# Hybrid layer in fp32: a chunk ahead in the feed-forward part, the first norm's residual on TensorE, w_out's last chunk by token halves

## The chip, the cores and the metric

The kernel runs on one core of a Trainium2 chip. The metric is the device time of one execution in microseconds (us). The engines are TensorE (PE; its weight loads PEld), VectorE (DVE), ScalarE (ACT), GpSimd (POOL) and SyncE (SP). DMAs are asked for on the queues of SP, ACT and POOL.

## The reference

One token batch of 256 tokens, model width 2048, feed-forward width 5632, all in fp32. Cut to what matters:

```python
def _mixer(x, w_in, ...):
    parts = jnp.split(x @ w_in, cuts, axis=-1)
    ...    # dilated attention -> ya; gated linear attention -> o
    ya = ya.reshape(b, s, A_WIDTH) @ w_proj_a
    o = o * lax.rsqrt(jnp.mean(o * o, axis=-1, keepdims=True) + LN_EPS) * gla_norm_g
    yb = (o.reshape(b, s, G_DV) * jax.nn.silu(gr)) @ w_proj_b
    y = jax.nn.sigmoid(m_a) * ya + jax.nn.sigmoid(m_b) * yb
    return y @ w_out

def _conv_ffn(x, w_gate, w_up, conv_w, conv_b, w_down):
    ...    # gc: 3-tap convolution of g = x @ w_gate over the tokens
    return (jax.nn.silu(gc) * (x @ w_up)) @ w_down

x = _layernorm(ALPHA * x + mix, ln1_g, ln1_b)
x = _layernorm(ALPHA * x + ffn, ln2_g, ln2_b)
```

## The kernel before

**Weights.** All weights come in pieces of 1 MB (128x2048, fp32), loaded by SP into `raw` (2 buffers) or `quarter` (6 buffers). `two_parts` splits a piece into two fp32r numbers: ScalarE writes the high one (`whi`, L136, 3 buffers) and VectorE the low one (`wlo`, L137, 2 buffers). TensorE then makes three products for each block of the operand: high by high, low by high and high by low (L228, L230 and L244, L247 for tiles; L260 to L262 for chunks). Every engine takes its instructions in order, so a split that stands behind something that waits is late, and TensorE with it.

**Units.** `seven` (L315) makes a block product with seven products instead of eight. It needs sums of weight pieces, made by accumulating DMAs on POOL's queue (`add_by_dma`, L345), or for the first v unit on VectorE (`add`, L342), and sums of operand quarters (`combine`, L292, instructions L301 to L304 on VectorE and their splits).

**Order.** The code is written as one list of work in which side work (attention, gates, sums) is dealt out by `pump` between weight pieces. A scheduler then fixes each engine's order before the run, from dependences and buffers; blocks of 128x512 come from one pool tag `blk`, with 14, 17 and 8 buffers in the pools early, late and last.

**The stages that the change touches.** (1) The v units run early. (2) In the late pool, `gated_out` (L830 to L840) makes sigmoid(gr) * gr * o for each head and both token halves and transposes the result for w_proj_b (L807), beside the product `yp` by w_proj_a. (3) `wo` is the product by w_out in four chunks of 512 columns, 16 operand blocks each, for both token halves; each chunk is followed by the residual (L902) and statistics (L903). (4) The first norm: mean and scale (L887 to L892), four products `keep` (L907), normalise (L915), 32 transposes (L923), gain and offset (L926), the operand split (L928, L931). The normalised `r` and the finished transposed `x1f` are spilled to DRAM. (5) The feed-forward part has six parts of 8, 8, 8, 8, 8 and 4 tiles of 128 columns. Part 0 runs as two groups of tiles (`fg`, `fu`, convolution L948 to L962), the next as one unit (`fgu`, four tiles) and one group. The unit of part p+1 is interleaved with the eight `step`s of the down-projection of part p: four chunks n of 512 columns with two weight pieces each, into the banks `wd_t` of both halves. A chunk's running sum `af` is fetched from DRAM at its first step (ACT's queue), added by `more` (L1029) and spilled (POOL's queue). In part 0, what is fetched is the normalised `r`, and `more` first applies the norm's gain and offset by two broadcast rows for each n (`row`, POOL's queue, and L1028 on VectorE).

## Time and profile before

| | |
|---|---|
| timed runs, median (lowest to highest) | 1941.08 us (1939.01 to 1942.84), 3 runs |
| the profiled execution's own time | 1931.08 us |
| its span | 1929.3 us |
| granted TensorE clock over the span | 0.981 |
| DMA moved | 480.45 MB, mean 249 GB/s |
| normalise, L915 on ScalarE | 8 of 0.80 us |
| weight splits on VectorE, L137 from quarter | 250 of 2.287 us |

How to read the rows that follow: a timeline row holds the start in us, the length in us, engine, line, operation, what is written <- what is read, shape, how many instructions of the kind follow each other, and in brackets how long the engine was idle before it and what ended that. A row of a group holds the count, then the busy time in us, the mean of one in ns, and the idle time before them by what ended it. A row of a DMA group holds the queue that issued it, the count, the size and the median time from issue to landing. Times count from the start of the span.

### The profile page before, as it was taken

The page shows a single profiled execution, that of the slowest core. Times are in us where ns is not written, and L with a number is a line of the kernel's source. Part 1 is how long each engine was busy: PE and PEld are TensorE (multiplying, and loading weights), DVE is VectorE, ACT ScalarE, POOL GpSimd, SP SyncE. Part 2 cuts the span into 40 slices and gives each one's busy share as a digit, 9 for nine tenths or more (in the row PEclk, how much of TensorE's full clock was granted, in tenths as well). Part 3 has the DMA queues.
Part 4 walks back from the last instruction along what each step waited for, and adds up shares of the span by engine and source line. Part 5 has one row for each costly group of instructions (what it writes and reads, how often), then busy time and mean ns, then how long its engine had stood idle before and what let it go on. Part 6 is the DMA issues. An engine that isn't in the chain of part 4 may idle for free.

```text
span 1929.3 us, 22786 instructions
## 1 busy us (share of the span) xinstructions
PE 1829.9 (95%) x8910; PEld 1523.0 (79%) x8910; DVE 1433.8 (74%) x1269; ACT 1020.0 (53%) x979; POOL 166.1 (9%) x270
## 2 busy tenths in 40 slices
PE   8989999999999999999999989887999999998996
PEld 6778887888888888887888868765887887887875
DVE  6979878878878797855755566675785786776877
ACT  6556555556665666545633345543554554554552
POOL 0001000001100111003100010010010000000101
PEclk9999999999999999999999989988999999999998
DMA  8469997987978879777765276668579587686783
GB/s 315 166 266 264 304 331 196 307 294 219 341 231 283 314 221 334 228 294 267 276 215 195 88 284 219 179 201 284 186 225 337 170 251 303 195 287 260 218 272 142
DMA packets 94920, 480.45 MB, mean 249 GB/s; under 512 B 11841, under 2 KB 22108, under 8 KB 46300
## 3 DMA queue, kind: packets, MB, share of 16 engines
q1 hardware_dynamic: 50252, 345.06, 47.6%
q0 software_dynamic: 22960, 107.08, 22.1%
q10 hardware_dynamic: 21600, 26.85, 4.3%
q8 instruction: 70, 1.15, 0.2%
q14 instruction: 38, 0.31, 0.0%
HBM read 385.55 MB, written 35.82 MB: 218 GB/s over the span
## 4 chain that ended last, share of the span: by engine, by line
PE 75%; DMA 10%; DVE 6%; issue 6%; ACT 2%; POOL 0%; SPq 0%; ACTq 0%; DVEq 0%; POOLq 0%
PE qk L228 8%; DMA raw<-in_wp 5%; PE fu L228 4%; PE qk L230 4%; DVE wlo L137 3%; PE fg L228 3%; PE wd_t L261 3%; PE wd_t L260 3%; PE wd_t L262 3%; PE fguD L329 2%; PE fu L230 2%; PE gqk L228 2%; PE fguA L329 2%; PE fg L230 2%; PE mD L329 2%
## 5 line engine op out<-in xcount | busy, mean ns | idle before, releaser
L137 DVE TENSOR_TENSOR wlo<-quarter,whi 128x2048 fp32r<-128x2048 f32 x250 | 571.0, 2287 | 182.3 <-ACT whi L136 73.1
L136 ACT ACTIVATE whi<-quarter 128x2048 fp32r<-128x2048 f32 x250 | 478.5, 1917 | 383.6 <-DVE quarter L342 89.5
L136 ACT ACTIVATE whi<-raw 128x2048 fp32r<-128x2048 f32 (+1 forms) x167 | 314.5, 1885 | 323.8 <-DMA raw<-in_wp 135.8
L137 DVE TENSOR_TENSOR wlo<-raw,whi 128x2048 fp32r<-128x2048 f32 (+1 forms) x167 | 375.8, 2250 | 123.5 <-ACT whi L136 52.8
L228 PE MATMUL qk<-x,whi 128*128 128x512 f32 x768 | 193.0, 399 | 1.5 <-ACT whi L136 1.5
L228 PEld LDWEIGHTS qk<-x,whi 128*128 128x128 f32 x768 | 142.0, 188 | 32.5 <-ACT whi L136 2.2
L342 DVE TENSOR_TENSOR quarter<-quarter,quarter 128x2048 f32<-128x2048 f32 x64 | 146.0, 2284 | 0.5
L261 PE MATMUL wd_t<-wlo,h 128*128 128x512 f32 x352 | 139.4, 396 | 5.6 <-DVE wlo L137 5.6
L260 PE MATMUL wd_t<-whi,h 128*128 128x512 f32 x352 | 138.2, 396 | 1.7 <-DVE af L1029 1.5
L262 PE MATMUL wd_t<-whi,h 128*128 128x512 f32 x352 | 138.3, 393 | 0.0
L345 POOL DMA_DIRECT2D quarter<-quarter x56 | 49.3, 880 | 665.5 <-DMA quarter<-in_wp 185.9
L230 PEld LDWEIGHTS qk<-x,wlo 128*128 128x128 f32 x768 | 98.4, 191 | 4.0 <-DVE wlo L137 0.3
L230 PE MATMUL qk<-x,wlo 128*128 128x256 f32 x768 | 99.7, 283 | 0.0
L228 PE MATMUL fu<-x,whi 128*128 128x512 f32 x368 | 89.7, 397 | 8.4 <-DVE pa L948 8.4
L228 PE MATMUL fg<-x,whi 128*128 128x512 f32 x352 | 88.0, 404 | 8.8 <-DVE af L1029 8.7
L228 PEld LDWEIGHTS fu<-x,whi 128*128 128x128 f32 x368 | 68.9, 192 | 22.3 <-issue 7.2
L228 PEld LDWEIGHTS fg<-x,whi 128*128 128x128 f32 x352 | 67.3, 196 | 23.4 <-issue 5.2
L261 PEld LDWEIGHTS wd_t<-wlo,h 128*128 128x128 f32 x352 | 67.1, 191 | 23.3 <-DVE wlo L137 9.4
L260 PEld LDWEIGHTS wd_t<-whi,h 128*128 128x128 f32 x352 | 67.0, 190 | 16.8 <-ACT h L136 1.7
L262 PEld LDWEIGHTS wd_t<-whi,h 128*128 128x128 f32 x352 | 67.0, 190 | 13.8
L228 PE MATMUL gqk<-x,whi 128*128 128x512 f32 x256 | 65.9, 407 | 4.4 <-ACT whi L136 4.1
L228 PEld LDWEIGHTS gqk<-x,whi 128*128 128x128 f32 x256 | 49.3, 196 | 17.7 <-ACT whi L136 7.7
(359 smaller groups left out, 3103.8 us busy)
## 6 DMA issues: line engine op xcount, KB each, us to landing
raw<-in_wp SPq DMA_DIRECT2D x163, 1024.0 KB, 5.1
quarter<-in_wp SPq DMA_DIRECT2D x160, 1024.0 KB, 11.1
quarter<-quarter POOLq DMA_DIRECT2D x56, 1024.0 KB, 12.2
af<-acc ACTq DMA_DIRECT2D x40, 256.0 KB, 13.0
acc<-af POOLq DMA_DIRECT2D x40, 256.0 KB, 5.2
sp<-c POOLq DMA_DIRECT2D x14, 256.0 KB, 10.6
bias<-bvd ACTq DMA_DIRECT2D x32, 96.0 KB, 4.8
v<-vs ACTq DMA_DIRECT2D x24, 128.0 KB, 2.9
```

The source lines that it names most:

```text
L136: nc.scalar.activation(hi, src, AF.Copy)
L137: nc.vector.tensor_tensor(lo, src, hi.bitcast(F32), op=ALU.subtract)
L228: nc.tensor.matmul(ps, parts(kc)[0], opnd(kc), start=(kc == 0), stop=False)
L230: nc.tensor.matmul(ps[:, S:], parts(kc)[1], opnd(kc)[:, :S], start=False, stop=(kc == nk - 1))
L260: nc.tensor.matmul(ps, xh, hi, start=first, stop=False)
L261: nc.tensor.matmul(ps, xh, lo, start=False, stop=False)
L262: nc.tensor.matmul(ps, xl, hi, start=False, stop=last)
L329: nc.tensor.matmul(ps, a(kc)[which], w[:, k * 512 : (k + 1) * 512], start=(first and w is hi and which == 0 and kc == 0), stop=(w is lo an ...
L342: tt(a, a, b, op=ALU.add)
L345: nc.gpsimd.dma_start(a, b, accum_op=ALU.add)
```

## The change

- **Sums.** In `combine` the operand quarters are got by a function; in the feed-forward part the getting of the blocks (`x1p`, four DMAs of 128x256 for each j) and the sums are two turns of the side work, and the turns are dealt out from the fourth tile of the first group on, not the eighth.
- **v.** The sums of weight pieces of the first v unit are accumulating DMAs too.
- **gated_out** is cut in three turns: fetch of head i, products of head i-1, transposes of head i-2.
- **w_out.** The last chunk runs by token halves: all four pieces are split first, then 48 matmuls for t=0 and 48 for t=1, each half followed by its norm (`normalised`). `keep` stands ahead of the second half's transposes. A spilled `x1f` is now 128x4x128 of one half; `r` is not spilled.
- **Residual.** In part 0 of the down-projection, TensorE adds the residual to `wd_t`: 8 fp32 matmuls for each n, x1f by `weighted`, which is ALPHA times the identity. `more` there is a copy of the bank on ScalarE and a spill. Rows and gain and offset on VectorE go.
- **Ahead.** `ahead(n + 1)` fetches a chunk's blocks at the first step of the chunk before.

```diff
@@ -296,7 +296,7 @@
...
             f = [tmp("comb").rearrange("p (k t) -> p k t", k=2) for _ in range(4)]
-            (a11, a21), (a12, a22) = ([raw[h][:, :, t * P : (t + 1) * P] for t in range(2)] for h in (j, j + 4))
+            (a11, a21), (a12, a22) = ([raw(h, t) for t in range(2)] for h in (j, j + 4))
             tt = nc.vector.tensor_tensor
@@ -405,11 +405,11 @@
...
     make_identity(nc, ident)
+    weighted = cpool.tile([P, P], F32, name="weighted")
+    nc.vector.tensor_scalar(weighted, ident, ALPHA, None, op0=ALU.mult)
     prm = cpool.tile([P, NPAR], F32, name="prm")
...
     pc = lambda c: prm[:, c : c + 1]
-    ones = cpool.tile([P, P], F32, name="ones")
-    nc.gpsimd.memset(ones, 1.0)
@@ -742,14 +742,14 @@
...
         for u in range(n):
-            yield from seven(name, X, comb, AT[name, u], sink(u), by_dma=(name, u) != ("v", 0))
+            yield from seven(name, X, comb, AT[name, u], sink(u), by_dma=True)
         yield lambda: passed.add(mark)
...
     next(tiles)()
-    comb, part = combine(X, XR)
+    comb, part = combine(X, lambda h, t: XR[h][:, :, t * P : (t + 1) * P])
     for j in range(4):
@@ -827,20 +827,31 @@
...
-    def gated_out(h):
+    got = {}
+    def gated_get(h):
+        got[h] = [(fetch("gr", GR[h][t]), fetch("o", O[h][t])) for t in range(2)]
+    def gated_mul(h):
+        for t, (x, o) in enumerate(got[h]):
+            sg = blk("sg")
+            nc.scalar.activation(sg, x, AF.Sigmoid)
+            nc.vector.tensor_tensor(x, x, o, op=ALU.mult)
+            nc.vector.tensor_tensor(sg, sg, x, op=ALU.mult)
+            got[h][t] = sg
+    def gated_stage(i):
         def f():
-            g = []
-            for t in range(2):
-                x, o = fetch("gr", GR[h][t]), fetch("o", O[h][t])
-                sg = blk("sg")
-                nc.scalar.activation(sg, x, AF.Sigmoid)
-                nc.vector.tensor_tensor(sg, sg, x, op=ALU.mult)
-                nc.vector.tensor_tensor(sg, sg, o, op=ALU.mult)
-                g.append(sg)
-            OB.extend(transposed("ob", h, g, P_NG))
+            if i < GH:
+                gated_get(i)
+            if 0 <= i - 1 < GH:
+                gated_mul(i - 1)
+            if 0 <= i - 2 < GH:
+                OB.extend(transposed("ob", i - 2, got[i - 2], P_NG))
         return f
-    side.extend(gated_out(h) for h in range(GH))
+    side.extend(gated_stage(i) for i in range(GH + 2))
     last_gate = []
@@ -892,44 +903,59 @@
...
+    def residual(n, t, ps):
+        r = R[t][n]
+        nc.vector.scalar_tensor_tensor(r, r, ALPHA, ps, op0=ALU.mult, op1=ALU.add)
+        nc.vector.bn_stats(stats[t][:, n, :], r)
+    X1 = [res("x1") for _ in range(4)]
+    X1F = [[None] * 4 for _ in range(2)]
+    def normalised(t):
+        _, rs, ms = mean_and_scale(t)
+        for n in range(4):
+            r = R[t][n]
+            nc.scalar.activation(r, r, AF.Identity, scale=rs, bias=ms)
+            pt = bank("pt")
+            x1 = blk("x1f").rearrange("p (k t) -> p k t", k=4)
+            for k in range(4):
+                nc.tensor.transpose(pt[:, k * P : (k + 1) * P], r[:, k * P : (k + 1) * P], ident)
+            for k in range(4):
+                d = 4 * n + k
+                nc.vector.tensor_scalar(x1[:, k], pt[:, k * P : (k + 1) * P], pc(P_L1G + d), pc(P_L1B + d), op0=ALU.mult, op1=ALU.add)
+            hi, lo = X1[n][:, :, t * P : (t + 1) * P], X1[n][:, :, S + t * P : S + (t + 1) * P]
+            main = nc.scalar.activation(hi, x1, AF.Copy)
+            nc.vector.tensor_tensor(lo, x1, hi.bitcast(F32), op=ALU.subtract)
+            X1F[t][n] = spill("x1s", x1)
+            if n == 2:
+                held = main
+        return held
+    yt = by_pairs(YT)
     for n in range(4):
...
             nc.gpsimd.dma_start(R[t][n], xk[t * P : (t + 1) * P, n * 512 : (n + 1) * 512])
-        pss = a_chunk("wo", by_pairs(YT), 16, AT["wo"] + 4 * n)
-        for t in range(2):
-            r = R[t][n]
-            nc.vector.scalar_tensor_tensor(r, r, ALPHA, pss[t], op0=ALU.mult, op1=ALU.add)
-            summed = nc.vector.bn_stats(stats[t][:, n, :], r)
-    norm = [mean_and_scale(t) for t in range(2)]
-    keep = bank("keep")
-    for _ in range(4):
-        nc.tensor.matmul(keep, ones, R[1][2], start=True, stop=True)
-    X1 = [res("x1") for _ in range(4)]
-    X1F = []
-    ACC = [[None] * 4 for _ in range(2)]
-    for n in range(4):
-        for t in range(2):
-            _, rs, ms = norm[t]
-            r = R[t][n]
-            nc.scalar.activation(r, r, AF.Identity, scale=rs, bias=ms)
-            ACC[t][n] = spill("acc", r)
-        for k in range(0, 4, 2):
-            pt = bank("pt")
-            x1 = blk("x1f")
-            for i in range(2):
-                for t in range(2):
-                    c = i * S + t * P
-                    nc.tensor.transpose(pt[:, c : c + P], R[t][n][:, (k + i) * P : (k + i + 1) * P], ident)
-                d = 4 * n + k + i
-                c = slice(i * S, (i + 1) * S)
-                nc.vector.tensor_scalar(x1[:, c], pt[:, c], pc(P_L1G + d), pc(P_L1B + d), op0=ALU.mult, op1=ALU.add)
-            hi, lo = X1[n][:, k : k + 2, :S], X1[n][:, k : k + 2, S:]
-            main = nc.scalar.activation(hi, x1.rearrange("p (k t) -> p k t", k=2), AF.Copy)
-            if n == 2:
-                held = main
-            nc.vector.tensor_tensor(lo, x1.rearrange("p (k t) -> p k t", k=2), hi.bitcast(F32), op=ALU.subtract)
-            X1F.append(spill("x1s", x1))
+        if n < 3:
+            pss = a_chunk("wo", yt, 16, AT["wo"] + 4 * n)
+            for t in range(2):
+                residual(n, t, pss[t])
+    pcs = [two_parts(load(AT["wo"] + 12 + k), spare=(k > 1)) for k in range(4)]
+    for t in range(2):
+        ps = cbank(f"wo_t{t}")
+        for k0 in range(4):
+            hi, lo = pcs[k0]
+            for k in range(4):
+                w = slice(k * 512, (k + 1) * 512)
+                kc = 4 * k0 + k
+                a_part(ps, yt(kc), hi[:, w], lo[:, w], t, kc == 0, kc == 15)
+        residual(3, t, ps)
+        if t:
+            keep = bank("keep")
+            for _ in range(4):
+                nc.tensor.matmul(keep, ident, R[0][2], start=True, stop=True)
+        held = normalised(t)
@@ -1017,16 +1044,21 @@
...
+        def ahead(n):
+            for t in range(2):
+                if part:
+                    st[n, t] = fetch("af", ACC[t][n], by=nc.scalar)
+                else:
+                    st[n, t] = fetch("x1f", X1F[t][n], lambda name: blk(name).rearrange("p (k t) -> p k t", k=4), by=nc.scalar)
         def more(n, pss):
             for t in range(2):
-                if last:
-                    a = F[t][:, n]
+                a = F[t][:, n] if last else st[n, t] if part else blk("wd0")
+                if part:
+                    nc.vector.tensor_tensor(a, a, pss[t], op=ALU.add)
                 else:
-                    a = st[n, t]
-                if not part:
-                    for i, op in ((2, ALU.mult), (3, ALU.add)):
-                        nc.vector.tensor_tensor(a, a, st["row", i], op=op)
-                nc.vector.scalar_tensor_tensor(a, a, 1.0 if part else ALPHA, pss[t], op0=ALU.mult, op1=ALU.add)
+                    nc.scalar.activation(a, pss[t], AF.Copy)
                 if last:
@@ -1037,17 +1069,21 @@
...
                     st["ps"] = [mbank(f"wd_t{t}") for t in range(2)]
+                    if n < 3:
+                        ahead(n + 1)
+                chunk_step(st["ps"], hk, nf, at, k0)
+                if not k0 and not part:
                     for t in range(2):
-                        st[n, t] = fetch("af", ACC[t][n], by=nc.scalar)
-                    if not part:
-                        for i in (2, 3):
-                            st["row", i] = row(i, n)
-                chunk_step(st["ps"], hk, nf, at, k0)
+                        for k in range(4):
+                            nc.tensor.matmul(
+                                st["ps"][t][:, k * P : (k + 1) * P], st[n, t][:, k], weighted, start=False, stop=False
+                            )
                 if k0 + 4 == nf:
...
         if not last:
+            ahead(0)
             return [step(n, k0) for n in range(4) for k0 in range(0, nf, 4)]
@@ -1067,14 +1103,18 @@
...
-    comb1, part1 = combine(X1, XF := {})
+    XF = {}
+    comb1, part1 = combine(X1, lambda h, t: XF[h, t])
     def sums(j):
-        def f():
+        def get():
             for h in (j, j + 4):
-                XF[h] = fetch("x1f", X1F[h], by=nc.scalar).rearrange("p (k t) -> p k t", k=2)
-            part1(j)
-        return f
+                pair = blk("x1p")
+                for t in range(2):
+                    b = pair[:, t * S : (t + 1) * S].rearrange("p (k t) -> p k t", k=2)
+                    nc.scalar.dma_start(b, X1F[t][h // 2][:, 2 * (h % 2) : 2 * (h % 2) + 2])
+                    XF[h, t] = b
+        return [get, lambda: part1(j)]
@@ -1084,11 +1124,11 @@
...
                     step()
+                    if not k and n == 3:
+                        side.extend(f for j in range(4) for f in sums(j))
                     if k or n > 3:
...
                             pump()
-                    if n == 7 and not k:
-                        side.extend(sums(j) for j in range(4))
         else:
```

In the unit of part 1, VectorE had the following before: the first chunk's residual instructions L1028 (on `af` and `row`) between the weight splits, and L1029 behind them.

```order
L137 TENSOR_TENSOR wlo_9507<-quarter_9420,whi_9506 128x2048
L1028 TENSOR_TENSOR af_9461<-af_9461,row_9465 128x512
L1028 TENSOR_TENSOR af_9463<-af_9463,row_9465 128x512
L137 TENSOR_TENSOR wlo_9523<-quarter_9422,whi_9522 128x2048
L1028 TENSOR_TENSOR af_9461<-af_9461,row_9467 128x512
L137 TENSOR_TENSOR wlo_9541<-raw_9538,whi_9540 128x2048
L1028 TENSOR_TENSOR af_9463<-af_9463,row_9467 128x512
L342 TENSOR_TENSOR quarter_9420<-quarter_9420,quarter_9578 128x2048
L342 TENSOR_TENSOR quarter_9422<-quarter_9422,quarter_9580 128x2048
L1029 SCALAR_TENSOR_TENSOR af_9461<-af_9461,wd_t_1128_9459 128x512
L1029 SCALAR_TENSOR_TENSOR af_9463<-af_9463,wd_t_1129_9460 128x512
```

Now, at the same place, the splits and the sums of weight pieces (L342) follow each other:

```order
L137 TENSOR_TENSOR wlo_9523<-quarter_9432,whi_9522 128x2048
L342 TENSOR_TENSOR quarter_9432<-quarter_9432,quarter_9592 128x2048
L137 TENSOR_TENSOR wlo_9539<-quarter_9434,whi_9538 128x2048
L342 TENSOR_TENSOR quarter_9434<-quarter_9434,quarter_9594 128x2048
L137 TENSOR_TENSOR wlo_9557<-raw_9554,whi_9556 128x2048
L137 TENSOR_TENSOR wlo_9602<-quarter_9432,whi_9601 128x2048
L137 TENSOR_TENSOR wlo_9618<-quarter_9434,whi_9617 128x2048
L137 TENSOR_TENSOR wlo_9643<-raw_9640,whi_9642 128x2048
```

The four L1028 and two L1029 rows are gone. On TensorE the residual stands behind the chunk's first weight piece, as products of `weighted` and the fetched blocks (two rows, one for each token half), ahead of the unit's next product `fguD`:

```order
L261 MATMUL wd_t_1123_9472<-wlo_9480,h_8727 128x512
L262 MATMUL wd_t_1123_9472<-whi_9479,h_8727 128x512
L1078 MATMUL wd_t_1122_9471<-weighted,x1f_9428 128x128 x4
L1078 MATMUL wd_t_1123_9472<-weighted,x1f_9430 128x128 x4
L329 MATMUL fguD_9521<-whi_9522,comb_1026_8598 128x512 x8
L329 MATMUL fguD_9521<-wlo_9523,comb_1026_8598 128x512 x4
```

On ScalarE the end of the second chunk of this down-projection is a copy of the two banks (L1061). The fetches of the blocks of the last chunk (L114) stand behind it, and weight splits (L136) before, between and behind:

```order
L136 ACTIVATE whi_9717<-raw_9715 128x2048
L136 ACTIVATE whi_9753<-quarter_9592 128x2048
L136 ACTIVATE whi_9769<-quarter_9594 128x2048
L1061 ACTIVATE wd_1149_9745<-wd_t_1138_9634 128x512
L1061 ACTIVATE wd_1151_9749<-wd_t_1139_9635 128x512
L114 DMA x1f_9788<-x1s_8469 128x512
L136 ACTIVATE whi_9794<-raw_9792 128x2048
L114 DMA x1f_9790<-x1s_8592 128x512
```

The copies were on VectorE as L1029; they now stand in the queue of the high splits. At the end of w_out TensorE had, before, the last matmuls of both halves, then keep and all transposes:

```order
L261 MATMUL wo_t_986_8326<-wlo_8420,yt_7913 128x512
L262 MATMUL wo_t_986_8326<-whi_8419,yt_7913 128x512
L907 MATMUL keep_8465<-r_8193,ones 128x512 x4
L923 MATMUL pt_8480<-ident,r_7931 128x128
L923 MATMUL pt_8492<-ident,r_7931 128x128
L923 MATMUL pt_8480<-ident,r_7933 128x128
```

Now a transpose group of the first half (four instructions, L923) stands between the matmuls of the second half (`wo_t_1009`):

```order
L261 MATMUL wo_t_1009_8471<-wlo_8338,yt_7657 128x512
L262 MATMUL wo_t_1009_8471<-whi_8337,yt_7657 128x512
L923 MATMUL pt_8412<-ident,r_7935 128x128 x4
L260 MATMUL wo_t_1009_8471<-whi_8337,yt_7657 128x512
L923 MATMUL pt_8427<-ident,r_8065 128x128 x4
L261 MATMUL wo_t_1009_8471<-wlo_8338,yt_7657 128x512
```

and behind the second half come keep, its transposes and the first feed-forward tiles:

```order
L260 MATMUL wo_t_1009_8471<-whi_8349,yt_7913 128x512
L261 MATMUL wo_t_1009_8471<-wlo_8350,yt_7913 128x512
L262 MATMUL wo_t_1009_8471<-whi_8349,yt_7913 128x512
L957 MATMUL keep_8522<-r_8195,ident 128x512 x4
L923 MATMUL pt_8535<-ident,r_7937 128x128 x4
L923 MATMUL pt_8550<-ident,r_8067 128x128 x4
L923 MATMUL pt_8565<-ident,r_8197 128x128 x4
L244 MATMUL fg_8620<-x_959_7931,whi_8604 128x512
L244 MATMUL fu_8621<-x_959_7931,whi_8610 128x512
```

So half of the transposes moved ahead of the last matmuls, and the first tiles `fg` and `fu` stand ahead of the last transpose group.

More of the change, by code (lines that the diff above doesn't have):

```diff
@@ L1012, in hybrid_layer @@
     F = []
+    ACC = [[None] * 4 for _ in range(2)]
     def down_group(part, nf, hs):
@@ L1115, in hybrid_layer @@
         older = down_group(part, nf, [h() for h in hs])
-    ACC = [[F[t][:, n] for n in range(4)] for t in range(2)]
     act_set(ACT_LN_EXP, held_by[0])
@@ L1121, in hybrid_layer @@
         for n in range(4):
-            a = ACC[t][n]
+            a = F[t][:, n]
             o = out[t * P : (t + 1) * P, n * 512 : (n + 1) * 512]
```

## The prediction

> **What bounds the kernel now.** I read the page first: span, busy shares, chain of work that ended last.
>
> ```profile
> span 1929.3 us, 22786 instructions
> PE 1829.9 (95%) x8910; PEld 1523.0 (79%) x8910; DVE 1433.8 (74%) x1269; ACT 1020.0 (53%) x979; POOL 166.1 (9%) x270
> PE 75%; DMA 10%; DVE 6%; issue 6%; ACT 2%; POOL 0%; SPq 0%; ACTq 0%; DVEq 0%; POOLq 0%
> ```
>
> TensorE is busy 1829.9 of 1929.3 us, so a change that removes no matmul can win at most the 99.4 us in which it idles, and the slow clock that follows an idle stretch. Next I read TensorE's timeline for rows with an idle time in brackets, around the lines that the diff touches.
>
> ```profile
> 906.20 0.66 PE L807 MATMUL pt<-ident,sg 128*128 128x128 f32 x2 [4.20 <-issue]
> 1118.71 0.39 PE L262 MATMUL wo_t<-whi,yt 128*128 128x512 f32 x1
> 1119.39 0.40 PE L262 MATMUL wo_t<-whi,yt 128*128 128x512 f32 x1
> 1119.63 3.60 PE L907 MATMUL keep<-r,ones 128*128 128x512 f32 x8
> 1127.11 0.44 PE L923 MATMUL pt<-ident,r 128*128 128x128 f32 x2 [3.88 <-ACT r L915]
> 1133.87 0.80 PE L244 MATMUL fg<-x,whi 128*128 128x512 f32 x1
> 1200.71 3.92 PE L228 MATMUL fu<-x,whi 128*128 128x512 f32 x16 [1.35 <-DVE pa L948]
> 1219.50 5.70 PE L228 MATMUL fu<-x,whi 128*128 128x512 f32 x16 [7.06 <-DVE pa L948]
> 1238.08 2.00 PE L329 MATMUL fguA<-whi,x 128*128 128x512 f32 x8
> 1262.12 2.07 PE L329 MATMUL fguD<-wlo,comb 128*128 128x512 f32 x4 [8.44 <-DVE wlo L137]
> 1314.99 2.08 PE L329 MATMUL fguA<-wlo,x 128*128 128x512 f32 x4 [7.37 <-DVE wlo L137]
> 1352.15 5.92 PE L228 MATMUL fg<-x,whi 128*128 128x512 f32 x16 [4.55 <-DVE af L1029]
> 1399.84 2.00 PE L329 MATMUL fguA<-whi,x 128*128 128x512 f32 x8
> 1487.11 3.91 PE L228 MATMUL fg<-x,whi 128*128 128x512 f32 x16 [0.26 <-DVE af L1029]
> ```
>
> The unit of part 1 of the feed-forward part runs from 1238.08 to 1352.15, 114.1 us; the same unit of part 2 from 1399.84 to 1487.11, 87.3 us. Both hold the same products and the same eight steps of the down-projection of the part before. The excess is 26.8 us. The windows of the two agree:
>
> ```profile
> 1238.00:1352.00 114.00, 90.17 (x371) 71.80 (x369) 74.87 (x58) 43.11 (x29) 11.08 (x18) 0.90 0.75 235
> 1400.00:1487.00 87.00, 84.87 (x369) 69.13 (x367) 65.01 (x41) 41.00 (x27) 6.75 (x10) 0.98 0.85 284
> ```
>
> (length, then TensorE, weight loads, VectorE, ScalarE, GpSimd, granted clock, DMA share, GB/s). TensorE has almost the same number of instructions; the clock is 0.90 against 0.98 and about 24 against 2 us are idle. What it waits for is a weight split on VectorE (wlo). Why VectorE is late stands in its own timeline:
>
> ```profile
> 1257.22 0.69 DVE L1028 TENSOR_TENSOR af<-af,row 128x512 f32<-128x512 f32 x1 [8.82 <-DMA af<-acc]
> 1311.45 0.69 DVE L1028 TENSOR_TENSOR af<-af,row 128x512 f32<-128x512 f32 x1 [11.40 <-DMA row<-in_rows]
> 1342.35 1.29 DVE L1028 TENSOR_TENSOR af<-af,row 128x512 f32<-128x512 f32 x2 [3.58 <-DMA row<-in_rows]
> 1347.91 1.29 DVE L1028 TENSOR_TENSOR af<-af,row 128x512 f32<-128x512 f32 x2 [4.27 <-DMA row<-in_rows]
> L1028 DVE TENSOR_TENSOR af<-af,row 128x512 f32<-128x512 f32 x16 | 10.5, 689 | 32.1 <-DMA row<-in_rows 22.0 <-DMA af<-acc 10.1
> L1029 DVE SCALAR_TENSOR_TENSOR af<-af,wd_t 128x512 f32<-128x512 f32 x40 | 27.3, 684 | 20.7 <-PE wd_t L262 20.7
> ```
>
> VectorE works in order; the 16 instructions of L1028 (gain and offset on the first norm's residual) hold it idle for 32.1 us until a spilled block or a broadcast row lands, and the splits stand behind them. That is the one large reserve that the change reaches.
>
> **The unit of part 1.** The 16 instructions of L1028 and the 8 broadcasts go. In their place come 32 fp32 matmuls of 128x128 by `weighted`, and 8 copies on ScalarE. No fp32 product of 128 columns into a running sum stands in the trace; the nearest rows are two.
>
> ```profile
> 229.81 0.39 PE L462 MATMUL ps<-qk 128*128 128x128 f32 x2
> 229.95 2.09 PE L329 MATMUL vB<-whi,comb 128*128 128x512 f32 x8
> ```
>
> Here one fp32 product of 128 columns (two instructions) starts 0.14 us ahead of its successor: 32 x 0.14 = 4.5 us. The keep row above has four fp32 products of 512 columns in 3.60 us, 0.90 each, a quarter for 128 columns: 0.225, 32 x 0.225 = 7.2 us. If 64 weight loads lay open at 0.19 us (71.80 us for 369 in the window) it would be 12. I take 7.2, since the keep row is eight instructions long and the other a single pair; both ends stay for the range. The Trainium skill, "FP8 and Floating Point Precision", section "TensorE Precision Notes", states that true FP32 takes four passes through the array; by it four passes of the usual pitch (1118.71 to 1119.39 is three matmuls, 0.227 us each) are 0.91 us for 512 columns, so it sides with 7.2 and against 4.5.
>
> ScalarE's copies are 8 of 128x512; the same shape in the norm takes 0.80 (row below), so 6.4 us on an engine that is busy 43.11 of 114 us: hidden. But each waits for the chunk's last matmul with the next piece's `whi` behind it. Pieces split ahead cover that, as they covered VectorE's wait for TensorE at L1029 (20.7 us over 40). Without that cover a chunk end costs one split, about 3 us, four times: 12 us, kept for the first rival.
>
> ```profile
> L915 ACT ACTIVATE r<-r,ms,rs 128x512 f32<-128x512 f32 x8 | 6.0, 800 | 2.3 <-DVE ms L892 2.3
> af<-acc ACTq DMA_DIRECT2D x40, 256.0 KB, 13.0
> acc<-af POOLq DMA_DIRECT2D x40, 256.0 KB, 5.2
> x1f<-x1s ACTq DMA_DIRECT2D x8, 256.0 KB, 5.1
> row<-in_rows POOLq DMA_DIRECT2D x8, 256.0 KB, 8.0
> quarter<-quarter POOLq DMA_DIRECT2D x56, 1024.0 KB, 12.2
> ```
>
> What is late next is a DMA. The x1f blocks now end on TensorE itself, but are asked for a chunk ahead, 87.3 / 4 = 22 us, against 13.0 to land at the worst median. The unit moved 235 GB/s x 114 us = 26.8 MB; eight rows of 256 KB (2.1 MB) go, and in 94.5 us the rest is 261 GB/s, below the 284 that the next unit had. So the unit comes to 87.3 + 7.2 = 94.5: **-19.6 us**, between -22.3 (4.5 us of matmuls) and -10 (12 us, and one wait of 5).
>
> The Trainium skill, "DMA: Bandwidth & Descriptors", section "Issuing engines are not separate DMA queues", says that transfers of all queues interleave on the same 16 engines. By it the fetch ahead makes nothing land faster where the engines are full; the trace, at a DMA share of 0.85, has 13.0 us for a block that takes 5.1 elsewhere, which agrees, and speaks for the first rival.
>
> **The tiles of part 0.** At 1200.71 and 1219.50 TensorE waits 1.35 and 7.06 us, and the 16 matmuls after the longer wait take 5.70 instead of 3.92: 10.2 us in all. VectorE was late there partly over the blocks for the weight sums:
>
> ```profile
> 1216.12 0.43 DVE L301 TENSOR_TENSOR comb<-x1f,x1f 128x256 f32<-128x256 f32 x1 [1.30 <-DMA x1f<-x1s]
> ```
>
> Now the sums start four tiles earlier, and a block's fetch is one turn ahead of its sums. VectorE's work is the same; it is spread over more tiles. Four waits of 1.3 us could stay: -6, between -10 and 0. **-6**.
>
> **The norm.** Before, from the last w_out matmul (1119.63) to the first of the feed-forward part (1133.87) pass 14.2 us, in which one chain runs: residual, statistics, mean and scale, normalise, 32 transposes.
>
> ```profile
> 1119.14 0.69 DVE L902 SCALAR_TENSOR_TENSOR r<-r,wo_t 128x512 f32<-128x512 f32 x1 [2.64 <-PE wo_t L262]
> 1126.06 0.14 DVE L892 SCALAR_TENSOR_TENSOR ms<-mv,rs 128x1 f32<-128x1 f32 x1
> ```
>
> The first token half takes 1126.06 - 1119.14 = 6.9 us to its scale, two splits of 2.3 us among them, and 1127.11 is its first transpose. In the new order t=0's first transposes stand 15 matmuls, 15 x 0.227 = 3.4 us (1118.71 to 1119.39 is three matmuls), into t=1's half, though the chain needs about 5.5 with one split: 2 us lost there. Behind t=1's half stands the same chain, 7.5 us to the first transpose, then half the transposes (6.8 us for 32 with their hand-overs, so 3.4). 2 + 7.5 + 3.4 = 12.9 against 14.2, and the eight spills of r leave the queue: **-2**, between -6 (no split in either chain) and +3 (two more).
>
> **The rest.** Adds become TENSOR_TENSOR at 0.69 for 0.68: nothing. In parts 1 to 4 L1029 waited only for TensorE, never for a block, so fetching earlier hides nothing there; at most the 2.1 us idle of each of four units (87.00 - 84.87) go, 8; at worst a pair fetched earlier delays one weight piece by its 5.1 us. **-2**, between -8 and +5.
>
> ```profile
> 118.34 1.20 PE L329 MATMUL vA<-wlo,x 128*128 128x512 f32 x4 [0.84 <-DVE wlo L137]
> L342 DVE TENSOR_TENSOR quarter<-quarter,quarter 128x2048 f32<-128x2048 f32 x64 | 146.0, 2284 | 0.5
> ```
>
> The first v unit's four sums leave VectorE (4 x 2.28 = 9.1 us) for accumulating DMAs at 12.2 us. VectorE is late for TensorE there by 0.84 and a like wait, -1.5 at best; a sum that comes 12.2 - 2.3 late would cost +10 in the product that uses it. These are used last in the unit: **0**, between -1.5 and +5.
>
> ```profile
> 905.41 0.69 DVE L838 TENSOR_TENSOR sg<-sg,o 128x512 f32<-128x512 f32 x1 [0.21 <-DMA o<-os]
> 908.94 0.69 DVE L838 TENSOR_TENSOR sg<-sg,o 128x512 f32<-128x512 f32 x1
> ```
>
> The 4.20 at 906.20 is the first gated block's wait. Its loads start no earlier, as its buffers come free no earlier; the transposes now stand behind 24 matmuls (5.4 us) but need both halves, 908.94 + 0.69 = 909.6 instead of 906.1. One undoes the other: **0**, between -4 and +3.5.
>
> **Sum:** -19.6 - 6 - 2 - 2 = -29.6 us. Against the profiled execution, 1929.3 becomes 1899.7 of span (1931.1 becomes 1901.5 with what lies around it). That execution is 9.6 us below the median of the three timed runs, 1941.1; from the median the time is **1911.5 us**.
>
> **Rivals.** First, *only the half*: the wait goes from VectorE to ScalarE and TensorE. Copy and whi stand in one queue, and x1f blocks land late among weight pieces. For it speaks 13.0 us at af<-acc and a DMA share of 0.75 to 0.85; against it the 22 us of lead. It costs the 12 us above and the 6 of the tiles: -29.6 + 18 = -11.6, 1929.5 us. Second, *all of it*: every stall that the diff touches goes, -22.3 - 10 - 6 - 8 - 1.5 - 4 = -51.8, 1889.3 us; the six do not depend on each other, so some four fifths of the way from the forecast, 1894 us, is as far as I take it. Third, *slower*: fetching ahead holds four of eight buffers of the last pool, so a fetch waits on ScalarE's queue until the spill of an older block has landed (5.2 us), and all weight splits stand behind it. There are 20 chunks in parts 0 to 4; at 2.6 us each, half a spill, it is 52 us, and the kernel ends at 1911.5 + 52 = 1963. It turns slower from 29.6 / 20 = 1.5 us a chunk. For it: one in-order queue. Against it: the order puts most fetches right behind the copies that free buffers. Fourth, *nothing*: TensorE would meet the accumulating DMAs where it met the rows, 1941; but the next units, with those DMAs and no rows, run in 87.3.
>
> **Chances.** Forecast 0.55 (1903 to 1921), half 0.24, all 0.11, slower 0.06, nothing 0.04. The range of 8 in 10 reaches from the second rival, as far as I take it, to the first: 1894 to 1929. About 0.2% (4 us) is what a measurement here can tell from no change. Faster 0.90, the same 0.04, slower 0.06.
>
> **What would show it.** In the profile after: the unit of part 1 near 94 us, clock near 0.98, no wait over 3 us on wlo; 64 fp32 instructions of 128x128 in some 7 us; in the tiles of part 0 no 7 us wait on pa; norm to first fg about 13 us; a wait of similar size still ahead of the first gated transposes. Wrong would be: ScalarE waiting for x1f's buffers or for wd_t with TensorE idle behind it, or TensorE waiting for x1f.

## The result, and the profile after

The changed kernel takes 1924.03 us, the median of 8 runs (1917.14 to 1932.83), against 1940.08 us before (8 runs): a ratio of 0.9924, 95% interval 0.9902 to 0.9946. That is 16 us faster; 29.6 us had been forecast (1911.5 from 1941.1). The time lies near the first rival (1929.5), but not for that rival's reason.

The page of the changed kernel shows what did not move: the share of TensorE (95% in both) and the DMA traffic (480.45 MB in both).

```profile
span 1922.2 us, 22923 instructions
PE 1835.5 (95%) x8974; PEld 1532.2 (80%) x8974; DVE 1413.9 (74%) x1258; ACT 1024.1 (53%) x987; POOL 160.8 (8%) x257
DMA packets 95368, 480.45 MB, mean 250 GB/s; under 512 B 11777, under 2 KB 24092, under 8 KB 46236
```

TensorE is busy 5.6 us longer in all (the new fp32 products alone take 7.8), VectorE 20 us less. Where the time went is read from TensorE's timeline, by the start of the first matmul of each stage. The table holds two profiled executions of each kernel; the second ones come from the experiments `before2` and `again` below.

| stage, from the first matmul of it to the first of the next | before, two profiles | changed, two profiles | difference of the means |
|---|---|---|---|
| start to yp | 887.8, 889.8 | 890.3, 892.8 | +2.8 |
| yp, with gated_out beside it | 54.1, 54.7 | 63.0, 62.2 | +8.2 |
| pb and wo, to keep | 177.8, 177.7 | 179.9, 179.9 | +2.2 |
| norm, keep to fg | 14.2, 14.3 | 11.4, 11.1 | -3.0 |
| tiles of part 0 | 104.2, 104.3 | 100.0, 93.4 | -7.6 |
| unit of part 1 | 114.1, 115.5 | 95.0, 94.8 | -19.9 |
| units of parts 2 to 4, sum | 261.4, 261.1 | 268.6, 267.6 | +6.9 |
| tiles of parts 1 to 4, sum | 191.1, 192.0 | 189.7, 190.3 | -1.6 |
| unit of part 5 to the last matmul | 107.1, 106.7 | 107.1, 109.5 | +1.4 |

The sum is -10.6 us, the medians differ by 16. The two profiled executions of the kernel before took 1931.1 and 1935.6 us, below its medians of 1938 to 1940, those of the changed kernel 1923.9 and 1920.2 at medians of 1924.0 and 1923.3; some 5 us are scatter of single executions, which the table cannot place.

The windows of the two units that the prediction set side by side, now (same columns as above):

```profile
1244.70:1339.80 95.10, 91.90 (x435) 76.69 (x433) 62.05 (x36) 46.59 (x36) 7.29 (x11) 0.98 0.80 257
1387.00:1476.00 89.00, 84.84 (x370) 69.29 (x368) 64.99 (x42) 42.00 (x28) 6.91 (x10) 0.98 0.85 278
```

The unit of part 1 has its full clock back and idles 3 us instead of 24. But the unit of part 2 idles 4 us where it idled 2. TensorE's timeline has the new waits:

```profile
910.95 0.30 PE L807 MATMUL pt<-ident,sg 128*128 128x128 f32 x1 [3.26 <-issue]
923.27 1.06 PE L807 MATMUL pt<-ident,sg 128*128 128x128 f32 x8 [2.33 <-DVE ob L815]
934.54 0.80 PE L261 MATMUL yp_t<-wlo,ya 128*128 128x512 f32 x1 [3.70 <-DVE wlo L137]
1140.84 1.84 PE L923 MATMUL pt<-ident,r 128*128 128x128 f32 x8 [3.99 <-ACT r L919]
1205.76 5.53 PE L228 MATMUL fg<-x,whi 128*128 128x512 f32 x16 [2.47 <-DVE pa L974]
1231.84 5.52 PE L228 MATMUL fg<-x,whi 128*128 128x512 f32 x16 [1.95 <-DVE pa L974]
1255.65 1.95 PE L1078 MATMUL wd_t<-weighted,x1f 128*128 128x128 f32 x16
1308.22 3.69 PE L329 MATMUL fguA<-whi,x 128*128 128x512 f32 x8 [3.20 <-ACT whi L136]
1448.11 3.68 PE L329 MATMUL fguA<-whi,x 128*128 128x512 f32 x8 [3.52 <-ACT whi L136]
```

Before, gated_out had one wait (4.20 at 906.20); now the stage has three, 9.3 us. And at the same place of the unit of part 1 and of part 2 TensorE waits over 3 us for a high split; parts 3 and 4 have 4.00 and 4.29. The chain of waits around 1448.11, in order of time (start, length, what), says why:

```profile
1431.34 14.29 DMA acc<-af
1445.63 0.02 issue
1445.65 0.02 ACTq L114
...
1445.70 0.33 ACTq L114
...
1446.15 1.92 ACT whi L136
1448.07 0.04 issue
1448.11 4.60 PE fguA L329 x12
```

A spill of a finished sum lands after 14.3 us. Only then is its buffer free, only then can ScalarE issue the fetch (L114) that stands at the head of its queue, and only behind that comes the split that TensorE needs. This is the mechanism of the third rival ("a fetch waits on ScalarE's queue until the spill of an older block has landed"), once in each unit. In the unit of part 1 it is a fetch of x1f that stands ahead of the split, on ScalarE's timeline:

```profile
1305.81 0.33 ACTq L114 DMA_DIRECT2D x1f<-x1s  x1
1306.26 3.71 ACT L136 ACTIVATE whi<-quarter 128x2048 fp32r<-128x2048 f32 x2 [11.45 <-issue]
acc<-wd POOLq DMA_DIRECT2D x2, 256.0 KB, 14.3
```

The last line is the pair of spills issued between 1290 and 1296; the first of them, from 1292.91, lands at 1305.75, just ahead of the fetch at 1305.81. So one of the prediction's signs of being wrong is there: "ScalarE waiting for x1f's buffers [...] with TensorE idle behind it", 3.20 us of it.

### The profile page after: what moved, and what is told of

Its sections match the earlier page's. It is cut to its first block, busy times and chain, and to the rows that moved or that the text cites. A ratio compares the mean times of both kernels' runs of the same rounds, so it can differ in the third digit from the quotient of the medians.

```text
span 1922.2 us, 22923 instructions
## 1 busy us (share of the span) xinstructions
PE 1835.5 (95%) x8974; PEld 1532.2 (80%) x8974; DVE 1413.9 (74%) x1258; ACT 1024.1 (53%) x987; POOL 160.8 (8%) x257
## 2 busy tenths in 40 slices
DMA packets 95368, 480.45 MB, mean 250 GB/s; under 512 B 11777, under 2 KB 24092, under 8 KB 46236
## 4 chain that ended last, share of the span: by engine, by line
PE 36%; DMA 8%; DVE 4%; issue 3%; ACT 2%; ACTq 0%; POOL 0%; POOLq 0%; DVEq 0%
PE fu L228 4%; DMA raw<-in_wp 3%; PE fguA L329 3%; PE fg L228 3%; PE wd_t L260 2%; PE wd_t L261 2%; PE wd_t L262 2%; DMA acc<-af 2%; DVE wlo L137 2%; PE fu L230 2%; PE fguD L329 2%; PE fg L230 2%; PE pb_t L262 2%; PE pb_t L260 2%; PE pb_t L261 2%
## 5 line engine op out<-in xcount | busy, mean ns | idle before, releaser
L136 ACT ACTIVATE whi<-quarter 128x2048 fp32r<-128x2048 f32 x250 | 477.9, 1915 | 391.0 <-DVE quarter L342 69.0
L136 ACT ACTIVATE whi<-raw 128x2048 fp32r<-128x2048 f32 (+1 forms) x167 | 314.0, 1883 | 270.2 <-DMA raw<-in_wp 126.9
L342 DVE TENSOR_TENSOR quarter<-quarter,quarter 128x2048 f32<-128x2048 f32 x60 | 137.1, 2286 | 0.6
L228 PE MATMUL fg<-x,whi 128*128 128x512 f32 x352 | 87.7, 403 | 5.3 <-DVE pa L974 4.4
## 6 DMA issues: line engine op xcount, KB each, us to landing
quarter<-quarter POOLq DMA_DIRECT2D x60, 1024.0 KB, 11.4
```

Of the source, the lines that this page charges most:

```text
L136: nc.scalar.activation(hi, src, AF.Copy)
L228: nc.tensor.matmul(ps, parts(kc)[0], opnd(kc), start=(kc == 0), stop=False)
L342: tt(a, a, b, op=ALU.add)
```

## The experiments

Theory 1 was, from these rows: the gain is the removal of L1028 and what goes with it, and it is partly given back in two places, by gated_out's three turns and by fetches ahead that want a buffer. The rivals: the losses are scatter, or contention of transfers.

**gated_out as before.** From the changed kernel:

```diff
...
-    side.extend(gated_stage(i) for i in range(GH + 2))
+    side.extend(gated_out(h) for h in range(GH))
```

> The changed kernel with gated_out as before (one turn per head, sg*gr then *o). Theory 1, the three stages cost what the stage yp lost in the two profiles (54.1 us before, 63.0 after, from the first yp matmul to the first pb matmul): the stage goes back to 54 to 56 us and the time falls by 7 to 9 us, to about 1916. Rival, the stage lost it because it began later and its loads met other transfers: the stage stays over 60 us and the time within 2 us of the changed kernel's 1924.

Measured: 1914.6 us, ratio 0.9870 (0.9848 to 0.9892); stage yp 54.7 us. The windows of 55 us from 890 on, of the changed kernel, of this one, and of the second profile of the kernel before:

```profile
890.00:945.00 55.00, 44.67 (x191) 35.05 (x190) 36.39 (x49) 36.03 (x54) 20.25 (x38) 0.91 0.82 294
890.00:945.00 55.00, 49.66 (x227) 40.09 (x226) 40.69 (x53) 37.64 (x57) 20.60 (x39) 0.97 0.93 332
890.00:945.00 55.00, 49.88 (x227) 40.25 (x226) 41.73 (x55) 39.37 (x59) 20.26 (x38) 0.97 0.91 330
```

With the old code TensorE runs 227 matmuls in the window, with the three turns 191. The stage began no earlier here (891.5 against 890.3) and moved more in the same time, 332 against 294 GB/s, so neither a late start nor crowded transfers had cost the time. Theory 1 holds: three turns cost 8 to 9 us.

**The old order of the products, in three turns** (the turns stay, sg*gr comes first again):

```diff
-            nc.vector.tensor_tensor(x, x, o, op=ALU.mult)
             nc.vector.tensor_tensor(sg, sg, x, op=ALU.mult)
+            nc.vector.tensor_tensor(sg, sg, o, op=ALU.mult)
```

> The changed kernel with gated_out in its three turns, but with the products in the old order (sg*gr as soon as gr is there, then *o). Theory 1a, the three turns cost, not the order of the products, since both halves have to be ready ahead of the first transposes and the next head's buffers come free later: stage yp stays 60 to 63.5 us. Theory 1b, the new order makes each product wait for o: stage yp falls to 54 to 57 us and the time by 6 to 9 us.

Measured: 1925.9 us, ratio 0.9928 (0.9912 to 0.9944); stage yp 63.7. The order of the products is not it.

**Two turns** (`gated_get(i)` and `gated_mul(i)` in one turn, the transposes in the next):

```diff
                 gated_get(i)
+                gated_mul(i)
             if 0 <= i - 1 < GH:
-                gated_mul(i - 1)
-            if 0 <= i - 2 < GH:
-                OB.extend(transposed("ob", i - 2, got[i - 2], P_NG))
+                OB.extend(transposed("ob", i - 1, got[i - 1], P_NG))
...
-    side.extend(gated_stage(i) for i in range(GH + 2))
+    side.extend(gated_stage(i) for i in range(GH + 1))
```

> The changed kernel with gated_out in two turns: fetch and products of head i, transposes of head i-1. Theory 1a', three heads in flight bunch the products, transposes and their copies, so that weight splits come late (3.70 us on wlo at 934.54): with two the stage yp is 55 to 59 us, the time 4 to 7 us below the changed kernel. Rival, what costs is that a head's transposes stand apart from its products and need both halves: stage 61 to 64 us, time as the changed kernel's.

Measured: 1921.3 us, ratio 0.9914 (0.9894 to 0.9935), which is not to be told from the changed kernel; stage yp 60.2, between the two expectations. One turn less brings back 2.4 us of the 8.2. ScalarE's timeline in the changed kernel shows a part of the bunching:

```profile
915.34 0.63 ACT L859 ACTIVATE m<-m 128x512 f32<-128x512 f32 x1 [5.93 <-DMA m<-sp]
915.88 1.90 ACT L136 ACTIVATE whi<-quarter 128x2048 fp32r<-128x2048 f32 x1
918.20 1.14 ACT L838 ACTIVATE sg<-gr 128x512 f32<-128x512 f32 x2
```

With three turns the activation for the gate of `yp` (m), which needs a block to be loaded, stands ahead of a high split and of the next head's sigmoids, and ScalarE waits 5.93 us for that block. In the profile of the kernel with gated_out as before nothing on ScalarE waits for m in this stage. The profiles together tell the two theories apart in part. In all seven with three turns ScalarE waits 5.8 to 5.9 us for m and TensorE 3.7 us for a late split, and the stage takes 62.2 to 63.7 us. With two turns ScalarE waits at most 0.81 us for m and TensorE 1.20 for a split, and the stage still takes 60.2, against 54.1 to 56.6 in the six profiles with one turn. So the bunching goes with the third turn and its 2.4 us; the larger rest stays without it, as the rival has it. That the rest is the transposes' need of both halves is not shown; one profile with two turns is what there is.

**The first v unit on VectorE again:**

```diff
-            yield from seven(name, X, comb, AT[name, u], sink(u), by_dma=True)
+            yield from seven(name, X, comb, AT[name, u], sink(u), by_dma=(name, u) != ("v", 0))
```

> The changed kernel with the first v unit's sums on VectorE again. Theory 1: the 2.6 us by which the first yp matmul comes later (887.75 before, 890.34 after) are the accumulating DMAs' doing; the matmul is back at 887 to 888 and the time falls by 2 to 3 us. Rival: it is scatter between executions; the matmul stays at 889 to 891 and the time within 1 us.

Measured: 1919.9 us, ratio 0.9890 (0.9873 to 0.9907); the first yp matmul at 890.9. By the matmul the rival is right; the time falls 4 us below 1924.0, which is nearer to theory 1, and the interval overlaps the changed kernel's second one. Over all 14 profiles the first yp matmul stands at 887.8, 889.8, 891.1 and 890.9 with these sums on VectorE (mean 889.9) and at 890.1 to 897.3 in the ten with DMAs (mean 893.0). That speaks for a loss of about 3 us, with a scatter (standard deviation) of 1.5 and 2.2; one run alone doesn't show it.

**The fetch ahead in part 0 alone:**

```diff
-                    if n < 3:
+                    if part:
+                        ahead(n)
+                    elif n < 3:
                         ahead(n + 1)
...
-            ahead(0)
+            if not part:
+                ahead(0)
```

> The changed kernel, with the fetch a chunk ahead in part 0 alone; from part 1 on each chunk's af is fetched at its own first step, as before. Theory 1, a fetch ahead stands on ScalarE's queue until a spill frees its buffer, with weight splits behind it: the units of parts 2 to 4 go from 89.2, 89.7 and 89.7 us back to 87.0 to 87.5, no TensorE wait over 3 us on whi is left in them, and the time falls by 6 to 8 us. Rival, the longer units come from the transfers: units stay over 89 and the time the same.

Measured: 1917.5 us, ratio 0.9882 (0.9862 to 0.9903); units of parts 2 to 4 at 86.9, 86.8 and 86.8 us. Theory 1 holds: fetching ahead costs 2 to 3 us a unit there and hides nothing. The longest wait of TensorE in these three units is 1.82 us, for a low split. In the unit of part 1, where the fetch ahead stayed, ScalarE still idles for 11.02 us ahead of a high split, there until products that read an older x1f are done.

**One buffer more** (the room taken from the small blocks):

```diff
-    now[:] = ctx.enter_context(tc.tile_pool(name="last", bufs=1)), (8, 9, 1)
+    now[:] = ctx.enter_context(tc.tile_pool(name="last", bufs=1)), (9, 7, 1)
```

> The changed kernel with 9 blk buffers in the last pool instead of 8 (and 7 tmp instead of 9, for the room). Theory 1, want of a buffer: ScalarE's idle of 11.4 us ahead of a whi, released by a spill's landing, shrinks or goes in the units of parts 1 to 4; units of 87 to 88 us, time down by 4 to 8 us. Rival, the fetch waits for something else, or fewer tmp buffers slow the sums in part 0's tiles: units unchanged, or part 0's tiles (100.0 us) longer.

Measured: 1911.7 us, ratio 0.9859 (0.9839 to 0.9879); units 90.0, 87.0, 86.6 and 87.4 us, part 0's tiles 100.4. ScalarE's timeline of this kernel at the place of the 11.4 us:

```profile
1440.09 1.92 ACT L136 ACTIVATE whi<-raw 128x2048 fp32r<-128x2048 f32 x1 [4.43 <-PE wd_t L262]
1441.91 1.91 ACT L136 ACTIVATE whi<-quarter 128x2048 fp32r<-128x2048 f32 x1
1444.62 1.92 ACT L136 ACTIVATE whi<-quarter 128x2048 fp32r<-128x2048 f32 x1 [0.80 <-PE fguA L329]
1446.61 0.33 ACTq L114 DMA_DIRECT2D af<-acc  x1
```

and of the changed kernel:

```profile
1432.86 1.90 ACT L136 ACTIVATE whi<-quarter 128x2048 fp32r<-128x2048 f32 x1
1445.70 0.33 ACTq L114 DMA_DIRECT2D af<-acc  x1
1446.15 1.91 ACT L136 ACTIVATE whi<-quarter 128x2048 fp32r<-128x2048 f32 x1 [11.39 <-DMA acc<-af]
```

The splits no longer wait behind a fetch: the scheduler, with a buffer more, has put it behind them. It was the buffer, not the transfers: the fetches ahead stayed, and the four units are together 12.6 us shorter. The time falls by 12 us, more than expected.

**The residual on TensorE alone**, in the kernel before, fetched at the chunk's first step:

```diff
...
-                    if not part:
-                        for i in (2, 3):
-                            st["row", i] = row(i, n)
...
+                if not k0 and not part:
+                    ...
+                            nc.tensor.matmul(
+                                st["ps"][t][:, k * P : (k + 1) * P], st[n, k // 2][:, c : c + P], weighted, start=False, stop=False
+                            )
```

> The kernel before with one part of the change alone: the first norm's residual added by TensorE (32 fp32 matmuls by weighted, copy on ScalarE, no rows, no spilled r), fetched at the chunk's first step as before. Theory 1, the removal of L1028 is the gain: unit of part 1 from 114.1 to 94 to 97 us, the other stages as before, time down by 17 to 20 us, to about 1921. Rival, the gain needs the fetch a chunk ahead: TensorE waits for x1f, unit over 103 us, time down by less than 11.

Measured: 1920.9 us, ratio 0.9904 (0.9889 to 0.9919); unit of part 1 98.1 us, part 0's tiles 105.3, norm 14.2, units of parts 2 to 4 at 86.9, 86.4 and 87.7. TensorE's timeline shows what the fetch ahead is for:

```profile
1257.10 2.24 PE L1049 MATMUL wd_t<-weighted,x1f 128*128 128x128 f32 x16 [1.08 <-DMA x1f<-x1s]
1309.65 2.93 PE L1049 MATMUL wd_t<-weighted,x1f 128*128 128x128 f32 x12 [3.31 <-DMA x1f<-x1s]
```

TensorE now waits itself for x1f, twice, as the rival had it, but the unit is 1 us above theory 1's bound and 5 below the rival's. So this part alone brings 16 to 17 us in its unit and, with 19 us, at least as much as the whole change in time. Against the units of the kernels that fetch ahead in part 0, 95.0 and with the ninth buffer 90.0, the fetch ahead adds 3, and with its buffer 8; those kernels differ in other parts too.

**The sums as before in time** (from the eighth tile on, got and summed in one turn):

```diff
...
-                    if not k and n == 3:
-                        side.extend(f for j in range(4) for f in sums(j))
...
+                    if n == 7 and not k:
+                        side.extend(sums(j) for j in range(4))
```

> The changed kernel with the sums of operand quarters from the eighth tile on, getting and sums in one turn, as before. Theory 1, the earlier start is what shortens part 0's tiles (104.2 and 105.3 us without it, 93.4 to 101.6 in the six profiles with it and 7 or more tmp): 103 to 106 us here, time up by 3 to 10 us, over 1927. Rival, the tiles are shorter because of the norm by halves or of scatter: under 101 us.

Measured: 1925.4 us, ratio 0.9933 (0.9914 to 0.9952); part 0's tiles 98.0 us. The rival is right: the early sums are not what shortened the tiles. The tiles scatter from 93.4 to 102.9 us in the eleven profiles with the norm by halves and the other form of the blocks (mean 98.1), and were 104.2 to 105.3 in the three without (mean 104.6). Two things can be read from the profiles. With the norm by halves 4 of the 32 transposes fall into this stage, without it 18: 14 instructions less, about 2 us by an estimate from their pitch of 0.14 us (two in 0.28 us at 1136.17 of the kernel before), which went to the last w_out chunk. And TensorE idles for 1.4 to 6.3 us in the eleven, 8.5 to 9.1 in the three. Whether the norm by halves shortened these waits too (its spills of x1f end earlier) or the other form of the blocks stays open.

**Both losses removed.** gated_out as before and the ninth buffer:

> The changed kernel with gated_out as before and 9 blk buffers (7 tmp). If the two losses are separate their gains add: stage yp 54 to 55, unit of part 1 about 90, units of parts 2 to 4 about 87; time 9 us (gated) and 8 us (4 units of 2 to 5) below the changed kernel, 1903 to 1909 us. Rival, one hides the other or the room for tmp is missed: over 1911 us.

Measured: 1907.0 us, ratio 0.9826 (0.9811 to 0.9840); stage yp 56.3, units 90.0, 87.2, 86.3 and 86.7. The time is in the range of theory 1 and the stage yp 1.3 us above it. The gains add for the most part: alone the two edits bring 9 and 12 us below 1924.0, together 17, a shortfall of 4 us that the intervals (3 to 4 us each way) don't settle. With the fetch ahead in part 0 alone:

> gated_out as before, 9 blk buffers, and the fetch a chunk ahead in part 0 alone. Theory 1, with a buffer more the fetch ahead neither costs nor gains from part 1 on: units of parts 2 to 4 at 86.5 to 87.5 and 1904 to 1910 us, as in best1 (1907.0). Rival, the fetch ahead gains there once it has its buffer: 1910 us or more here.

Measured: 1904.6 us, ratio 0.9824 (0.9807 to 0.9840). The two are not to be told apart, so with a buffer more the fetch ahead is worth nothing from part 1 on. Both beat both kernels: 33 us below the one before, twice the gain of the change.

**Each kernel once more.**

> The changed kernel itself once more. It shows what a second profile of the same code differs by, stage by stage: theory 1 has the stage yp at 62 to 63.5 us and the units of parts 2 to 4 at 88.5 to 90 us again, and the part of the time up to the first yp matmul (887.8 before; 890.3, 891.5, 890.9, 890.1 and 894.5 us in five profiles with the change) as scatter of a few us. Time 1920 to 1927 us. Rival, stages too scatter by as much as was read from them (9 us in the stage yp).

Measured: 1923.3 us, ratio 0.9922 (0.9900 to 0.9944). The stage yp (62.2) and the units (89.0, 89.1 and 89.5) are where theory 1 has them. All stages repeat within 1 us but for the start (2.5 us), the last unit (2.4) and part 0's tiles (100.0 and 93.4).

> The kernel before once more, for a second profile of it. Theory 1, its first profile (span 1929.3, 9 us under the median) was a quick execution in stages that the change doesn't touch: the first yp matmul comes at 890 to 894 us instead of 887.8, the last unit to the end takes 107 to 110, while unit 1 is 113 to 116 again. Rival, the change gains more in the stages it touches than the first pair of profiles shows: unit 1 or part 0's tiles over 118 or 108 us.

Measured: 1938.9 us, ratio 1.0004 (0.9990 to 1.0019). Theory 1 is right about the touched stages (unit 1 at 115.5, tiles 104.3), and misses its ranges for the rest by a little: yp comes at 889.8, the end takes 106.7.

## Why the prediction was right, and where it was not

**The unit of part 1** (-19.6, from 87.3 + 7.2): 95.0 and 94.8 us, -19.9. The price of the products is near the one chosen, 7.2 us. The group in the changed kernel:

```profile
L1078 PE MATMUL wd_t<-weighted,x1f 128*128 128x128 f32 x64 | 7.8, 275 | 0.0
```

7.8 us in four runs of 1.95, or 0.24 for each of the 32 products, so the fp32 product of 128 columns costs about what a quarter of a 512-column one does (0.225 by the keep row), and the weight loads hide. The -19.9 has two errors that cancel, and that they do is luck: one wait of 3.20 with slow matmuls behind it was not foreseen, and without it (the kernels with one buffer more) the unit is 90.0, not 94.5. The 4.5 us were in the 87.3 taken as a floor. Here are the unit that gave the floor (part 2 of the kernel before) and the unit of part 1 with the ninth buffer:

```profile
1399.84:1487.11 87.27, 85.03 (x371) 69.32 (x369) 65.17 (x41) 41.27 (x27) 6.90 (x10) 0.98 0.85 283
1248.20:1338.18 89.98, 89.95 (x435) 75.34 (x433) 61.99 (x36) 46.77 (x36) 7.25 (x11) 1.00 0.81 272
```

The first holds 2.2 us of idle time, and a granted clock of 0.98 against 1.00 is, by an estimate from the row, another 1.7 us; the second has neither. The copies on ScalarE cost nothing that can be seen: TensorE idles for 0.03 us in that unit.

**The tiles of part 0** (-6): -4 and -11, mean -7.6, and -6.5 by the means over all 14 profiles; but not by the step named. The early sums do nothing that can be measured.

**The norm** (-2): -3.0 in the norm itself and +2.2 in pb and wo, together near -0.9. That the prediction had "2 us lost there" is luck. It meant a wait of TensorE for the first half's chain, said to need 5.5 us where 15 matmuls cover 3.4. There is no such wait: TensorE idles for 0.02 us in the whole stage, and the first transpose starts at 1123.81, 3.4 us after the half's residual (1120.43), with no split between them. The 2.2 us are the first half's transposes themselves:

```profile
L923 PE MATMUL pt<-ident,r x16: 270/272/329, 1123.8 to 1128.8; 128*128 128x128 f32 x16
```

The prediction also took the 6.8 us behind 1127.11 for 32 transposes. They held 14; the other 18 stood among the first `fg` and `fu`, so most of the 2.2 us came out of the tiles of part 0, and the gain there is smaller by as much.

**The rest, fetch ahead** (-2, between -8 and +5): +6.9 in the units of parts 2 to 4, outside the bounds. "At worst a pair fetched earlier delays one weight piece by its 5.1 us" left out that a fetch can stand on the queue and hold the splits. The step that failed is the price of the third rival: "the spill of an older block has landed (5.2 us)" and "the order puts most fetches right behind the copies that free buffers". Most do; one a unit doesn't, and its spill, issued among weight pieces, lands after 14.3 us, not the 5.2 of the median. One wait in each of four units lies between none and the rival's one in each of 20 chunks.

**gated_out** (0, between -4 and +3.5): +8.2, outside the bounds. The step compared only the first head, 909.6 against 906.1 with 24 matmuls of cover. The first wait did shrink, 4.20 to 3.26. But the later heads cost more: 2.33 us ahead of the second head's transposes, and a late split (3.70). The bound was taken from one head of four.

**The first v unit** (0, between -1.5 and +5): about +3 by the profiles, within its bounds, not settled.

So the mechanism of the main term was right and its size too; two terms, put at 0 and at -2, gave back 15 us of it. That the time lies within the range is luck in part: the upper end was set by a rival that did not occur as priced (12 us of copies in the way of splits in part 1, and no gain in the tiles), and the room left for it was used up by two other losses.

## What to carry to other kernels

A prefetch is worth what its consumer waits for, and needs a buffer of its own: fetched earlier into the same pool, it waits for that pool, and whatever stands behind it on the queue that issues it waits too. Look for the longest landing of the spill that frees the buffer (here 14.3 us), not for the median (5.2). And when a step is cut into pipeline stages, cost all its repetitions, not the first: here the gain was in one wait and the loss in the later ones.

## What the runs showed of the hardware that was not expected

The clock falls after idle times shorter than I had thought. At 1231.84 in the changed kernel TensorE had idled 1.95 us, and its next 16 matmuls took 5.52 us where 16 behind a wait of 1.35 took 3.92 (row 1200.71 of the kernel before): here a wait of 2 us costs 3.6. The waits of 3.20 and 3.52 us cost the same 1.7 us on top (8 matmuls in 3.68 instead of 2.00); behind those of 4.00 and 4.29 the next four matmuls are slow too (1.91 and 1.83 us instead of 1.09). The Trainium skill, "TensorE: Matmul & The Clock Gate", section "Part 1: The HAM clock gate", puts the fall to half clock at one idle window of about 3.4 us; here 1.95 us was enough. Not every wait of this length does it, as a row of the kernel with the sums as before in time shows:

```profile
1754.34 3.88 PE L228 MATMUL fg<-x,whi 128*128 128x512 f32 x16 [2.47 <-DVE af L1059]
```

From 900 us on, no wait under 1.8 us ahead of 512-column matmuls was followed by such slow ones in any of the 14 profiles; of those between 1.8 and 3 us some were and some weren't.

The same spill of 256 KB lands after 4.7 us in the median of the changed kernel, and after 13.9 us as the median of two at 1431 and 1434, beside weight pieces. The DMA issues of the window from 1428 to 1448 us:

```profile
quarter<-in_wp SPq DMA_DIRECT2D x3, 1024.0 KB, 15.9
quarter<-quarter POOLq DMA_DIRECT2D x1, 1024.0 KB, 15.1
...
acc<-af POOLq DMA_DIRECT2D x2, 256.0 KB, 13.9
```

Here a small transfer issued among 1 MB ones took nearly as long as they did.
